# A hybrid mixer and mixture-of-experts block: modulation buffers, the zero fill, two orders of issue, and the accumulators of the tail

## The chip, the cores and the metric

The kernel runs on one core of one Trainium2 chip. The metric is the device time of one execution in microseconds (us). Before the change it is 1450.79 us, the median of 3 runs (1450.4 to 1452.89).

## The reference

One layer of a hybrid block over 512 latent tokens of width 1024 with a prefix of 256 context tokens, in float32. Cut to what matters here:

```python
sh1, sc1, g1, sh2, sc2, g2 = modulation(c, w_mod, b_mod, 6)      # silu(c) @ w_mod + b_mod
cm = modulation(c_ctx, w_mod, b_mod, 2)
hc = rmsnorm(ctx) * (1 + cm[1]) + cm[0]
hx = rmsnorm(x) * (1 + sc1) + sh1
# p = h @ w_in: retention k, v; delta-net k, v behind a conv of length 3; decays and betas ("gates"); queries
sol = triangular_solve(a + I, [beta*v, beta*exp(g)*k])            # per chunk of 128 tokens, head, direction
x = x + g1 * rmsnorm(mixer_out(retention(...), delta_net(...), ...))
h2 = rmsnorm(x) * (1 + sc2) + sh2
x = x + g2 * rmsnorm(moe(h2))                                     # 64 experts, 8 per token, and a shared one
```

The context tokens only supply the first states of the scans. In the mixture of experts each token's eight expert outputs are weighted and summed.

## The kernel before, in words

The program is written phase by phase against a framework that hands out buffers from pools, sets the semaphores, and lists the instructions of each engine; every engine then works off its own list in order, and a DMA's issue is an instruction in the list of the engine that issues it (SP for most loads). A buffer that is reused makes its next writer wait.

Float32 products are done as three matmuls of a high and a low part (`mm3`, lines 111 to 113). The high part is a cast (`hi_of`, mostly on ACT, line 100), the low part a subtraction (`lo_of`, line 107, on DVE or POOL). A unit of weights is a raw tile of 512 KB (`raw`, three buffers, line 148) and its two parts (`wu`, four buffers in a ring that `gcv` shares, so three for weights).

*Modulation (phase0, to about 64 us).* Sixteen tiles `wm` of w_mod of 512 KB each, line 300, in five buffers (three of `raw`, two of a pool of their own); matmuls into four accumulators; x and ctx normalised (POOL does x, line 286), transposed (lines 330 and 338), and turned into `hTc` and `hTx`.

*State features (phaseG, to about 350 us).* First two context projections in units of two rows of 128 (`rcA`, `rcB`, copied at line 415). At its start ACT issues a DMA that fills the DRAM buffer `zd` (1.5 MB) with zeros, from a tile of 258 columns (line 382); `zd` later receives the inverse's blocks. Then 16 columns of gates (`gT`, lines 434 and 435, transposed at line 439), and twelve convolution blocks: four of keys, four of values, four of queries, each a projection (`projT`) followed by short ACT and DVE work (lines 494 to 501). `prep(t)` builds for each of six chunks a decayed product `CT` and stores it to `cd`; two small transposes of `br` go to `bd` (lines 528 to 534). `base()` loads both back as `M` and `bb` and inverts 32 x 32 triangles on DVE, step by step. Behind the value blocks, transposes at line 717 make `vtok`.

*Retention, output projection (phaseR, phaseO), then the experts (phaseM, about 740 to 1417 us).* Each expert loads three weights of 1 MB on SP (line 1178; the last slot, a spill-over expert, by POOL gathers at line 1176), multiplies, and POOL scatters its result `y` with addition into one of two DRAM accumulators `accd[0]`, `accd[1]` (line 1258). They alternate, except that the last four slots (61 to 64) all go to `accd[1]`, which lets `accd[0]` (`m0`) and half of the block's input (`x1`) be loaded in iteration 62 of the loop. A second loop (`cnt` passes, none for these inputs) follows, then the *tail*: load `accd[1]` in four tiles, add `m0`, take the mean square (ACT), its power -0.5 (`rsqrt`: one DVE instruction, one POOL power), scale, add to the output.

Of the kernel before, what the change touches and what calls it, by code (L numbers as in the profile page):

```python
# [9 lines left out]
F32 = mybir.dt.float32  # L10
F32R = mybir.dt.float32r
# [3 lines left out]
OP = mybir.AluOpType  # L15
# [56 lines left out]
class K:  # L72
# [128 lines left out]
    def run(self, upto="end"):  # L201
        nc, tc, a = self.nc, self.tc, self.a
        main = self.main = self.pool("main")
        self.pes = ExitStack()
        self.psum = self.pool("ps", es=self.pes, space=PSUM)
        self.wi = a["w_in"][0].rearrange("(k p) n -> p k n", p=128)
        self.ident = main.tile([128, 128], F32, name="ident")
        self.mhalf = main.tile([128, 1], F32, name="mhalf")
        nc.vector.memset(self.mhalf, -0.5)
        self.vecT = main.tile([128, 68], F32, name="vecT")  # L210
        self.sc = main.tile([128, 8], F32, name="scc")
        self.keep = self.pool("keep")
        self.rawp = self.pool("raw", bufs=3)
        self.w8 = {"a": self.pool("w8a", bufs=4)}
        self.pat, self.wn, self.pre = "a", 0, {}
        self.hxs, self.gcs, self.hcs = ExitStack(), ExitStack(), ExitStack()
        self.ctx.callback(self.hxs.close)
        p = self.pool("hxp", side="right", es=self.hxs)
        self.hxpool = p
        self.hTx = p.tile([128, 8, 512], F32R, name="hTx", tag="b0")  # L220
        self.hLx = p.tile([128, 8, 512], F32R, name="hLx", tag="b1")
        self.gc = self.pool("gc", side="right", es=self.gcs)
        p = self.pool("hcp", side="right", es=self.hcs)
        self.hTc = p.tile([128, 8, 256], F32R, name="hTc")
        self.hLc = p.tile([128, 8, 256], F32R, name="hLc")
        self.phase0()
        if upto == "0":
            for s in (self.hcs, self.gcs, self.hxs, self.pes):
                s.close()
            return  # L230
        self.phaseG()
        self.phaseR()
        if upto == "R":
            self.w8s.close()
            self.hxs.close()
            self.pes.close()
            return
        self.phaseO()
        self.phaseM()


    def phase0(self):
# [50 lines left out]

        pm = [self.pa(), self.pa(), self.pa(), self.pc()]
        wv = a["w_mod"][0].rearrange("(p k) n -> p k n", k=8)
        for k in range(8):
            for hf in range(2):
                i = k * 2 + hf
                w = (self.rawp if i % 5 < 3 else wp).tile([128, 1024], F32, name="wm", tag="raw")
                nc.sync.dma_start(w, wv[:, k, hf * 1024:hf * 1024 + 1024])  # L300
                if k < 7:
                    wu = self.wt8([128, 2, 1024], F32R, "wmu")
                    wh, wl = wu[:, 0], wu[:, 1]
                    self.hi_of(wh, w, "act")
                    self.lo_of(wl, w, wh)
                for q in range(2):
                    s = slice(q * 512, q * 512 + 512)
                    o = pm[hf * 2 + q][0:2]
                    if k < 7:
                        self.mm3(o, sch[:, k], scl[:, k], wh[:, s], wl[:, s], k == 0, False)  # L310
                    else:
                        nc.tensor.matmul(o, sc[:, k], w[:, s], start=False, stop=True)
# [14 lines left out]
        for k in range(8):  # L327
            pc = self.pc()
            for t in range(2):
                nc.tensor.transpose(pc[:, t * 128:t * 128 + 128], xs[4 + t][:, k * 128:k * 128 + 128], self.ident)  # L330
            h = wp.tile([128, 256], F32, name="hc")
            nc.vector.tensor_scalar(h, pc[:, 0:256], modT[:, 8 + k, 1:2], modT[:, k, 1:2], op0=OP.mult, op1=OP.add)
            self.hi_of(self.hTc[:, k], h, "act")
            self.lo_of(self.hLc[:, k], h, self.hTc[:, k])
        for k in range(8):
            px = self.pi()
            for t in range(4):
                nc.tensor.transpose(px[:, t * 128:t * 128 + 128], xs[t][:, k * 128:k * 128 + 128], self.ident)
            h = wp.tile([128, 512], F32, name="h", tag="h")
            nc.scalar.activation(h, px, AF.Identity, scale=modT[:, 8 + k, 0:1], bias=modT[:, k, 0:1])  # L340
            self.hi_of(self.hTx[:, k], h, "pool")
            self.lo_of(self.hLx[:, k], h, self.hTx[:, k])
# [3 lines left out]
    def phaseG(self):  # L346
# [30 lines left out]

        cd_, zd, bd = dp.tile([6, 4, 16512], F32, name="cd"), dp.tile([6, 4, 16512], F32, name="zd"), dp.tile([2, 24, 128], F32, name="bd")
        gd = dp.tile([48, 128], F32, name="gd")
        zero = gp.tile([128, 258], F32, name="zero", tag="E")  # L380
        nc.gpsimd.memset(zero, 0.0)
        nc.scalar.dma_start(zd.rearrange("t h n -> (t h n)").rearrange("(p a n) -> p a n", p=128, n=258), zero[:, None, :].to_broadcast([128, 12, 258]))
        plane = lambda d, t: bass.AP(tensor=d.tensor, offset=d.offset + t * 66048, ap=[[128, 128], [16512, 4], [1, 128]])
        blocks = lambda d, t0, t1: bass.AP(tensor=d.tensor, offset=d.offset + t0 * 66048, ap=[[4128, (t1 - t0) * 16], [128, 32], [1, 32]])
        tri = gc.tile([128, 2, 128], F32, name="tri")
# [45 lines left out]

        px, pc = self.projT(2048, n=16, ctx=True)
        gT = gc.tile([16, 768], F32, name="gT", tag="vq")
        nc.scalar.copy(gT[:, 0:512], px[0:16])
        nc.scalar.copy(gT[:, 512:768], pc[0:16, 0:256])
        pt = self.pc()
        for t in range(6):
# [48 lines left out]
        nc.scalar.activation(kts, kts, AF.Exp)  # L486


        def conv(b, dx, dc):
            cv = lambda j: self.vecT[:, 24 + j * 12 + b:25 + j * 12 + b]  # L490
            r = self.projT({0: 3088, 1: 1024, 2: 1536}[b // 4] + (b % 4) * 128, ctx=dc is not None, lo="dve" if b // 4 == 1 else "pool")
            for ps, dst, n in ((r, dx, 512),) if dc is None else ((r[0], dx, 512), (r[1], dc, 256)):
                t = ctile()
                nc.scalar.activation(dst, ps[:, 0:n], AF.Identity, scale=cv(1))
# [29 lines left out]
        for l in range(2):  # L524
            nc.vector.tensor_scalar(nD[:, l], br[:, :, 4:8], even[:, l:l + 1], None, op0=OP.mult)
            stt(nD[:, l], br[:, :, 0:4], odd[:, l:l + 1], nD[:, l], op0=OP.mult, op1=OP.add)
        for dr in range(2):
            ps = self.pc()
            brd = gc.tile([128, 6, 4], F32, name="brd", bufs=2)
            nc.vector.tensor_copy(brd, br[:, :, dr * 4:dr * 4 + 4])  # L530
            nc.tensor.transpose(ps[0:24, 0:128], brd.rearrange("p t h -> p (t h)"), self.ident)
            bt = gc.tile([24, 128], F32, name="bt", bufs=2)
            nc.scalar.copy(bt, ps[0:24, 0:128])
            nc.sync.dma_start(bd[dr], bt)

        ZT, QE, CTs = {}, {}, {}

        def prep(t):
# [158 lines left out]
                        self.d("gdn_o", fl(zz), t - 2)  # L697
                    ptt(o, o, bj(c), op=OP.mult)

        for t in range(6):  # L700
            prep(t)
        gps.close()
        bps = ExitStack()
# [7 lines left out]
        vc = gcv[:, 2:4].rearrange("p a (h d) -> p (a h) d", h=2)  # L711
        for h in range(4):
            conv(8 + h, vx[:, h], vc[:, h])
        for t in range(6):
            pk = self.pc()
            for h in range(4):
# [6 lines left out]

        qx = gc.tile([128, 4, 512], F32, name="qx", tag="vq")
        for h in range(4):
            conv(h, qx[:, h], None)
        pq = self.pc()
        for h in range(4):
            sq = ctile()
# [413 lines left out]
    def phaseM(self):  # L1143
# [258 lines left out]
        for e in range(NE + 2):  # L1402
# [9 lines left out]
                convert(e + 2, 0)  # L1412
            make(e + 2, 0)
            if e > 0:
                down(aT, SL[e - 1], W[e - 1], raw(e - 1, 2), 1 if e - 1 > NE - 4 else (e - 1) % 2)
                load(e + 2, 2)
            make(e + 2, 1)
            prepare(e + 4)
            if e == NE - 2:

                halves = lambda w: [w[:, i * 1024:i * 1024 + 1024] for i in range(2)]
                m0 = halves(raw(e, 0)) + halves(raw(e, 1))
                x1 = halves(raw(e + 1, 0)) + halves(raw(e + 1, 1))
                for t in range(4):
                    nc.sync.dma_start(m0[t], self.accd[0][t * 128:t * 128 + 128])
                for t in range(2, 4):
                    nc.sync.dma_start(x1[t], self.out[t * 128:t * 128 + 128])


        cnt = nc.values_load(nx[0:1, 0:1], min_val=0, max_val=62)  # L1430
        with tc.For_i(0, cnt) as _:
# [7 lines left out]
            pgu = self.pa()  # L1439
            for n in range(2):  # L1440
                proj(pgu[:, n * 256:n * 256 + 256], [xT[:, h] for h in range(2)], w[n])
            down(turn_act(act(pgu[:, 0:256], pgu[:, 256:512])), ix, ws, raw(NE, 2), 1)


        m = halves(raw(NE, 0)) + halves(raw(NE, 1))
        r = q.tile([128, 4], F32, name="fr")
        for t in range(4):
            (nc.scalar if t % 2 else nc.sync).dma_start(m[t], self.accd[1][t * 128:t * 128 + 128])
        for t in range(4):
            tt(m[t], m[t], m0[t], op=OP.add)  # L1450
            self.d("moe", m[t], t)
            junk = q.tile([128, 1024], BF, name="xT", bufs=2)
            nc.scalar.activation(junk, m[t], AF.Square, accum_out=r[:, t:t + 1])
            self.rsqrt(r[:, t:t + 1], r[:, t:t + 1], 1.0 / D, EPS)
        for t in range(4):
            nc.vector.scalar_tensor_tensor(m[t], m[t], r[:, t:t + 1], g2p, op0=OP.mult, op1=OP.mult)
            if t < 2:
                nc.gpsimd.dma_start(self.out[t * 128:t * 128 + 128], m[t], accum_op=OP.add)
            else:
                tt(m[t], m[t], x1[t], op=OP.add)  # L1460
                (nc.scalar if t % 2 else nc.sync).dma_start(self.out[t * 128:t * 128 + 128], m[t])
        self.pes.close()

# [20 lines left out]
```

## Time and profile before

| | before |
|---|---|
| median of 3 runs | 1450.79 us |
| profiled execution | 1450.15 us, span 1448.4 us, so 1.75 us around it |
| busy share | PE 92%, DVE 62%, ACT 45%, POOL 28% |
| chain that ended last, by engine | PE 66%, DVE 8%, DMA 8%, POOL 2% |
| DMA engines by stage | full from about the middle of the span, 350 to 370 GB/s there |

The chain is followed back from the last instruction to what released it. The page also shows the span in 40 slices of 36 us; each digit is a busy share in tenths, for PEclk the clock that TensorE was granted (9 is 90% or more of 2.4 GHz, 5 is half), for DMA the mean busy share of its 16 engines:

```profile
PE   6989888899999999997799999999999999999991
PEclk9899999999999999999899999999999999999995
DMA  8643421102226578566388999999999999999954
```

TensorE has its thinner slices at the very start, between 72 and 290 us and at 650 to 725 us, and does next to nothing in the last one; the DMA engines have theirs from 72 to about 430 us.

### The profile page before, as it was taken

To read this page: it belongs to the slowest core of one execution; us is meant where nothing else is said; L and a number is where in the kernel's file an instruction comes from. 1 tells how busy PE (TensorE), PEld (TensorE's weight loads), DVE (VectorE), ACT (ScalarE), POOL (GpSimd) and SP (SyncE) were. 2 spreads that over 40 slices of the span, in tenths; PEclk is the share of its full clock that TensorE was granted. 3 is DMA by queue.
4 is the path that set the end of the run, shared out by engine and by line. 5 is a ranking of instruction groups with operands and counts; after the bars stand their busy time and mean duration, and the time that the engine had idled before them with its cause. 6 is when DMAs were issued, how large, how long until landed. Compare 5 with 4: busy or idle time off the path is not lost.

```text
span 1448.4 us, 20720 instructions
## 1 busy us (share of the span) xinstructions
PE 1338.8 (92%) x7848; PEld 1085.2 (75%) x7848; DVE 901.3 (62%) x1268; ACT 655.7 (45%) x927; POOL 404.1 (28%) x330
## 2 busy tenths in 40 slices
PE   6989888899999999997799999999999999999991
PEld 2668776898887767776678787878787878888770
DVE  5635695566777556557366666666666666666543
ACT  5534442543323223244145655555555555555531
POOL 0414644855330000012022222222222222223312
PEclk9899999999999999999899999999999999999995
DMA  8643421102226578566388999999999999999954
GB/s 283 191 106 107 125 58 41 44 16 84 78 69 203 177 212 232 167 248 245 136 282 295 351 364 347 367 354 347 364 357 361 362 362 357 368 353 353 327 184 124
DMA packets 138841, 340.51 MB, mean 235 GB/s; under 512 B 28218, under 2 KB 84574, under 8 KB 113780
## 3 DMA queue, kind: packets, MB, share of 16 engines
q1 hardware_dynamic: 110952, 289.46, 56.5%
q0 software_dynamic: 19584, 38.99, 10.7%
q10 hardware_dynamic: 8204, 10.72, 2.4%
q8 instruction: 63, 1.03, 0.3%
q14 instruction: 38, 0.31, 0.1%
HBM read 326.59 MB, written 48.31 MB: 259 GB/s over the span
## 4 chain that ended last, share of the span: by engine, by line
PE 66%; DVE 8%; DMA 8%; POOL 2%; issue 2%; ACT 1%; SPq 0%; ACTq 0%; DVEq 0%; POOLq 0%
PE cs L1253 15%; PE acc L113 12%; PE acc L112 12%; PE acc L111 12%; PE ci L1222 4%; DMA raw<-in_w_in_dram 2%; PE ci L1056 2%; DMA wd<-in_w_down_dram 2%; DVE wu L107 1%; PE acc L1242 1%; PE acc L1067 1%; DMA mraw<-in_w_mod_dram 1%; ACT wu L100 1%; PE ci L596 1%; PE cs L655 1%
## 5 line engine op out<-in xcount | busy, mean ns | idle before, releaser
L111 PE MATMUL acc<-wh,xT 128*128 128x256 f32 x1040 | 304.9, 293 | 0.0
L113 PE MATMUL acc<-wh,xT 128*128 128x256 f32 x1040 | 294.4, 283 | 0.0
L112 PE MATMUL acc<-wl,xT 128*128 128x256 f32 x1040 | 294.1, 283 | 0.0
L1158 DVE TENSOR_TENSOR wl<-w,wh 128x2048 fp32r<-128x2048 f32 x88 | 201.6, 2291 | 87.4 <-PE acc L112 86.0
L1253 PE MATMUL cs<-wd,aT 128*128 128x512 f32 x520 | 235.8, 596 | 2.9 <-DMA wd<-in_w_down_dram 2.1
L1258 POOL DMA_INDIRECT acc<-y,slots x64 | 101.9, 1592 | 474.7 <-ACT y L1255 427.4
L1156 ACT CAST wh<-w 128x2048 fp32r<-128x2048 f32 x88 | 167.3, 1901 | 100.7 <-PE acc L113 85.6
L111 PEld LDWEIGHTS acc<-wh,xT 128*128 128x128 f32 x1040 | 199.6, 192 | 0.2 <-issue 0.2
L112 PEld LDWEIGHTS acc<-wl,xT 128*128 128x128 f32 x1040 | 199.4, 192 | 0.2 <-issue 0.2
L113 PEld LDWEIGHTS acc<-wh,xT 128*128 128x128 f32 x1040 | 198.8, 191 | 0.0
L1253 PEld LDWEIGHTS cs<-wd,aT 128*128 128x128 f32 x520 | 94.5, 192 | 97.6 <-issue 96.6
L1225 DVE TENSOR_TENSOR xT<-ci,xT 128x512 fp32r<-128x512 f32 x130 | 89.1, 686 | 89.7 <-ACT xT L1224 89.6
L100 ACT CAST wu<-raw 128x1024 fp32r<-128x1024 f32 (+1 forms) x73 | 74.9, 1036 | 113.4 <-DMA raw<-in_w_in_dram 74.1
L1158 DVE TENSOR_TENSOR wl<-wgu,wh 128x2048 fp32r<-128x2048 f32 x42 | 96.3, 2292 | 41.5 <-PE acc L112 41.4
L111 PE MATMUL acc<-hTx,wu 128*128 128x512 f32 (+1 forms) x296 | 119.2, 403 | 1.9 <-ACT wu L100 1.9
L113 PE MATMUL acc<-hTx,wu 128*128 128x512 f32 (+1 forms) x296 | 118.4, 400 | 1.5 <-DVE wu L107 1.5
L112 PE MATMUL acc<-hLx,wu 128*128 128x512 f32 (+1 forms) x296 | 117.9, 398 | 0.0
L107 DVE TENSOR_TENSOR wu<-raw,wu 128x1024 fp32r<-128x1024 f32 (+1 forms) x61 | 77.1, 1270 | 64.6 <-ACT wu L100 63.5
L1156 ACT CAST wh<-wgu 128x2048 fp32r<-128x2048 f32 x42 | 79.7, 1898 | 50.0 <-PE acc L113 42.1
L1222 PEld LDWEIGHTS ci<-ident,xg 128*128 128x128 f32 x520 | 73.4, 192 | 29.8 <-issue 29.5
L1214 POOL DMA_INDIRECT xg<-h2d,slots x64 | 71.3, 1113 | 31.6 <-issue 18.0
L1222 PE MATMUL ci<-ident,xg 128*128 128x128 f32 x520 | 80.0, 278 | 0.0
(492 smaller groups left out, 2371.6 us busy)
## 6 DMA issues: line engine op xcount, KB each, us to landing
wd<-in_w_down_dram SPq DMA_DIRECT2D x64, 1024.0 KB
w<-in_w_gate_dram SPq DMA_DIRECT2D x43, 1024.0 KB
w<-in_w_up_dram SPq DMA_DIRECT2D x43, 1024.0 KB
raw<-in_w_in_dram SPq DMA_DIRECT2D x56, 512.0 KB
wgu<-in_w_gate_dram SPq DMA_DIRECT2D x21, 1024.0 KB
wgu<-in_w_up_dram SPq DMA_DIRECT2D x21, 1024.0 KB
mraw<-in_w_mod_dram SPq DMA_DIRECT2D x32, 512.0 KB
wm<-in_w_mod_dram SPq DMA_DIRECT2D x16, 512.0 KB
```

Of the source, the lines that this page charges most:

```text
L100: nc.scalar.copy(dst, src)
L107: (self.nc.gpsimd if eng == "pool" else self.nc.vector).tensor_tensor(dst, src, hi.bitcast(F32), op=OP.subtract)
L111: mm(out, ah, bh, start=start, stop=False)
L112: mm(out, ah, bl, start=False, stop=False)
L113: mm(out, al, bh, start=False, stop=stop)
L1156: nc.scalar.copy(h[:, i:i + max(n, 1024)], w[:, i:i + max(n, 1024)])
L1158: eng(l[:, i:i + n], w[:, i:i + n], h[:, i:i + n].bitcast(F32), op=OP.subtract)
L1214: nc.gpsimd.indirect_dma_start(xg[:, :], None, self.h2d[:, :], bass.IndirectOffsetOnAxis(ap=ix, axis=0), bounds_check=511, oob_is_err=False)
L1222: nc.tensor.transpose(ps[:, k * 128:k * 128 + 128], xv[:, :, c * 4 + k], self.ident)
L1225: tt(l, ps, h.bitcast(F32), op=OP.subtract)
L1253: nc.tensor.matmul(ps, aT[:, m], wd[:, s], start=k == 0, stop=k == 1)
L1258: nc.gpsimd.indirect_dma_start(self.accd[acc][:, :], bass.IndirectOffsetOnAxis(ap=sx, axis=0), y[:, :], None, bounds_check=511, oob_is_err ...
```

## The change

Five parts.

1. Modulation weights: tiles 3 to 10 get eight buffers in the space that `hTx` and `hLx` take later; the others use the three `raw` buffers; the pool of two is used for them no more.
2. Zero fill: the source is now 774 columns of `gcv`, set to zero on POOL, so a packet has 3096 bytes instead of 1032; the DMA is issued on ACT right behind the first copy of `gT`.
3. `prep(0)` and `prep(1)` come ahead of the two transposes of `br`.
4. The projection of the first query block comes ahead of the transposes to `vtok`.
5. Tail: scatters alternate to the end, extra passes go to `accd[0]`; `accd[1]` is loaded in iteration 64 (`m1`) and x1 with it, `accd[0]` at the end; the last root is a bias on ACT (a constant tile `eps`) and a power on POOL.

```diff
@@ -209,0 +210,2 @@
+        self.eps = main.tile([128, 1], F32, name="eps")
+        nc.vector.memset(self.eps, EPS)
@@ -220,2 +221,0 @@
-        self.hTx = p.tile([128, 8, 512], F32R, name="hTx", tag="b0")
-        self.hLx = p.tile([128, 8, 512], F32R, name="hLx", tag="b1")
@@ -295,0 +296 @@
+        wms = [t[:, i] for t in [self.hxpool.tile([128, 4, 1024], F32, name="wm", tag=tag) for tag in ("b0", "b1")] for i in range(4)]
@@ -299 +300 @@
-                w = (self.rawp if i % 5 < 3 else wp).tile([128, 1024], F32, name="wm", tag="raw")
+                w = wms[i - 3] if 3 <= i < 11 else self.rawp.tile([128, 1024], F32, name="wm", tag="raw")
@@ -334,0 +336,2 @@
+        self.hTx = self.hxpool.tile([128, 8, 512], F32R, name="hTx", tag="b0")
+        self.hLx = self.hxpool.tile([128, 8, 512], F32R, name="hLx", tag="b1")
@@ -380 +383 @@
-        zero = gp.tile([128, 258], F32, name="zero", tag="E")
+        zero = gcv[:, 2:4].rearrange("p a n -> p (a n)")[:, 0:774]
@@ -382 +384,0 @@
-        nc.scalar.dma_start(zd.rearrange("t h n -> (t h n)").rearrange("(p a n) -> p a n", p=128, n=258), zero[:, None, :].to_broadcast([128, 12, 258]))
@@ -434 +436,2 @@
-        nc.scalar.copy(gT[:, 0:512], px[0:16])
+        with tc.issue_after(nc.scalar.copy(gT[:, 0:512], px[0:16]).ins):
+            nc.scalar.dma_start(zd.rearrange("t h n -> (t h n)").rearrange("(p a n) -> p a n", p=128, n=774), zero[:, None, :].to_broadcast([128, 4, 774]))
@@ -489 +492,4 @@
-        def conv(b, dx, dc):
+        def conv_in(b, ctx):
+            return self.projT({0: 3088, 1: 1024, 2: 1536}[b // 4] + (b % 4) * 128, ctx=ctx, lo="dve" if b // 4 == 1 else "pool")
+
+        def conv(b, dx, dc, r=None):
@@ -491 +497,2 @@
-            r = self.projT({0: 3088, 1: 1024, 2: 1536}[b // 4] + (b % 4) * 128, ctx=dc is not None, lo="dve" if b // 4 == 1 else "pool")
+            if r is None:
+                r = conv_in(b, dc is not None)
@@ -527,9 +533,0 @@
-        for dr in range(2):
-            ps = self.pc()
-            brd = gc.tile([128, 6, 4], F32, name="brd", bufs=2)
-            nc.vector.tensor_copy(brd, br[:, :, dr * 4:dr * 4 + 4])
-            nc.tensor.transpose(ps[0:24, 0:128], brd.rearrange("p t h -> p (t h)"), self.ident)
-            bt = gc.tile([24, 128], F32, name="bt", bufs=2)
-            nc.scalar.copy(bt, ps[0:24, 0:128])
-            nc.sync.dma_start(bd[dr], bt)
-
@@ -700 +698,11 @@
-        for t in range(6):
+        prep(0)
+        prep(1)
+        for dr in range(2):
+            ps = self.pc()
+            brd = gc.tile([128, 6, 4], F32, name="brd", bufs=2)
+            nc.vector.tensor_copy(brd, br[:, :, dr * 4:dr * 4 + 4])
+            nc.tensor.transpose(ps[0:24, 0:128], brd.rearrange("p t h -> p (t h)"), self.ident)
+            bt = gc.tile([24, 128], F32, name="bt", bufs=2)
+            nc.scalar.copy(bt, ps[0:24, 0:128])
+            nc.sync.dma_start(bd[dr], bt)
+        for t in range(2, 6):
@@ -713,0 +722 @@
+        q0 = conv_in(0, False)
@@ -726 +735 @@
-            conv(h, qx[:, h], None)
+            conv(h, qx[:, h], None, q0 if h == 0 else None)
@@ -1415 +1424 @@
-                down(aT, SL[e - 1], W[e - 1], raw(e - 1, 2), 1 if e - 1 > NE - 4 else (e - 1) % 2)
+                down(aT, SL[e - 1], W[e - 1], raw(e - 1, 2), (e - 1) % 2)
@@ -1419 +1428 @@
-            if e == NE - 2:
+            if e == NE:
@@ -1422,4 +1431,2 @@
-                m0 = halves(raw(e, 0)) + halves(raw(e, 1))
-                x1 = halves(raw(e + 1, 0)) + halves(raw(e + 1, 1))
-                for t in range(4):
-                    nc.sync.dma_start(m0[t], self.accd[0][t * 128:t * 128 + 128])
+                m1 = halves(raw(e - 2, 0)) + halves(raw(e - 2, 1))
+                x1 = halves(raw(e - 1, 0))
@@ -1427 +1434,3 @@
-                    nc.sync.dma_start(x1[t], self.out[t * 128:t * 128 + 128])
+                    nc.sync.dma_start(x1[t - 2], self.out[t * 128:t * 128 + 128])
+                for t in range(4):
+                    nc.sync.dma_start(m1[t], self.accd[1][t * 128:t * 128 + 128])
@@ -1442 +1451 @@
-            down(turn_act(act(pgu[:, 0:256], pgu[:, 256:512])), ix, ws, raw(NE, 2), 1)
+            down(turn_act(act(pgu[:, 0:256], pgu[:, 256:512])), ix, ws, raw(NE, 2), 0)
@@ -1448 +1457 @@
-            (nc.scalar if t % 2 else nc.sync).dma_start(m[t], self.accd[1][t * 128:t * 128 + 128])
+            (nc.scalar if t % 2 else nc.sync).dma_start(m[t], self.accd[0][t * 128:t * 128 + 128])
@@ -1450 +1459 @@
-            tt(m[t], m[t], m0[t], op=OP.add)
+            tt(m[t], m[t], m1[t], op=OP.add)
@@ -1453,2 +1462,4 @@
-            nc.scalar.activation(junk, m[t], AF.Square, accum_out=r[:, t:t + 1])
-            self.rsqrt(r[:, t:t + 1], r[:, t:t + 1], 1.0 / D, EPS)
+
+            nc.scalar.activation(junk, m[t], AF.Square, scale=D ** -0.5, accum_out=r[:, t:t + 1])
+            nc.scalar.activation(r[:, t:t + 1], r[:, t:t + 1], AF.Identity, bias=self.eps)
+            nc.gpsimd.tensor_tensor(r[:, t:t + 1], r[:, t:t + 1], self.mhalf, op=OP.pow)
@@ -1460 +1471 @@
-                tt(m[t], m[t], x1[t], op=OP.add)
+                tt(m[t], m[t], x1[t - 2], op=OP.add)
```

What this does to the lists of the engines, at three places.

ACT's list from the first units of weights (`wu`) to the gate copies (`gT`); `zd` is the buffer filled with zeros, `rcA` and `rcB` are context projections. Before:

```order
L100 CAST wu<-raw 128x1024 x2
L382 DMA zd<-zero 1536x1x258
L415 COPY rcA<-acc 128x512 x2
L100 CAST wu<-raw 128x1024 x2
L100 CAST wu<-raw 128x128
L415 COPY rcB<-acc 128x512 x2
L434 COPY gT<-acc 16x512
L435 COPY gT<-acc 16x256
```

and now:

```order
L100 CAST wu<-raw 128x1024 x2
L417 COPY rcA<-acc 128x512 x2
L100 CAST wu<-raw 128x1024 x2
L100 CAST wu<-raw 128x128
L100 CAST wu<-raw 128x1024
L417 COPY rcB<-acc 128x512 x2
L100 CAST wu<-raw 128x1024
L436 COPY gT<-acc 16x512
L437 DMA zd<-gcv 512x1x774
L438 COPY gT<-acc 16x256
```

The DMA to `zd` moved from ahead of the copies of `rcA` to between the two gate copies, and two casts of weights come ahead of the gates.

POOL's list at the end of the preparation: `QE3` to `QE5` are decay factors of the last chunks, `W` the inverse's work area, `wu_1597` (now `wu_1592`) the weights of a value convolution. Before:

```order
L550 TENSOR_TENSOR QE3_1231<-QE3_1231,rk_1083 128x512
L565 MEMSET W_1296 96x2048
L550 TENSOR_TENSOR QE4_1250<-QE4_1250,rk_1083 128x512
L550 TENSOR_TENSOR QE5_1269<-QE5_1269,rk_1083 128x512
L568 MEMSET W_1296 96x32 x2
L107 TENSOR_TENSOR wu_1597<-raw_1595,wu_1597 128x512 x2
```

and now:

```order
L548 TENSOR_TENSOR QE3_1226<-QE3_1226,rk_1078 128x512
L107 TENSOR_TENSOR wu_1592<-raw_1590,wu_1592 128x512 x2
L563 MEMSET W_1291 96x2048
L548 TENSOR_TENSOR QE4_1245<-QE4_1245,rk_1078 128x512
L548 TENSOR_TENSOR QE5_1264<-QE5_1264,rk_1078 128x512
L566 MEMSET W_1291 96x32 x2
```

The weight's two halves (x2) moved ahead of the memset of `W` and of the last two decay products.

SP's list at the end of the program: `wd` are down-projection weights, `wgu<-acc` and `w<-acc` loads of an accumulator, `w<-out_dram` loads of x; the branches are the second loop. Before:

```order
L1178 DMA wd<-in_w_down_dram 128x2048 x3
L1425 DMA wgu<-acc_4923 128x1024 x4
L1427 DMA w<-out_dram 128x1024 x2
L1431 COMPARE_AND_BRANCH
L1431 UNCONDITIONAL_BRANCH x2
L1479 BRANCH_PREFETCH_HINT
L1431 REGISTER_ALU
L1431 COMPARE_AND_BRANCH
L1431 UNCONDITIONAL_BRANCH
L1448 DMA w<-acc_4924 128x1024 x2
```

and now:

```order
L1187 DMA wd<-in_w_down_dram 128x2048 x2
L1434 DMA w<-out_dram 128x1024 x2
L1187 DMA wd<-in_w_down_dram 128x2048
L1436 DMA wgu<-acc_4919 128x1024 x3
L1440 COMPARE_AND_BRANCH
L1440 UNCONDITIONAL_BRANCH x2
L1490 BRANCH_PREFETCH_HINT
L1440 REGISTER_ALU
L1440 COMPARE_AND_BRANCH
L1440 UNCONDITIONAL_BRANCH
L1436 DMA wgu<-acc_4919 128x1024
L1457 DMA w<-acc_4918 128x1024 x2
```

Before, all four loads of `accd[0]` and then x stand behind the weights. Now x stands ahead of the last of them, three loads of `accd[1]` behind it and one behind the loop, ahead of the loads of `accd[0]`.

## Rows read from the trace of the kernel before

**Rows 1.** Waits, 5 to 41 us. Columns: waiter, what it waited for, total us, times, longest.
```profile
ACT wmu L100 <- DMA wm<-in_w_mod_dram: 9.0, 9, 4.1
ACT junk L282 <- DMA x<-in_x_dram: 3.2, 1, 3.2
```

**Rows 2.** Busy time by engine in two stretches: us (x instructions), granted clock, DMA share, GB/s.
```profile
13.40:40.00 26.60, 25.59 (x92) 7.79 (x92) 16.43 (x16) 14.64 (x20) 0.92 (x2) 1.00 0.88 311
48.00:52.00 4.00, 3.96 (x15) 3.46 (x16) 3.48 (x7) 3.45 (x6) 1.24 (x2) 0.50 0.42 120
```

**Rows 3.** Waits, 40 to 110 us, TensorE for the normalised x.
```profile
PE ci L338 <- POOL x L286: 2.0, 3, 0.7
```

**Rows 4.** Timeline of ACT: start, us, engine, line, operation, [idle before <-releaser].
```profile
63.51 0.59 ACTq L382 DMA_DIRECT2D zd<-zero  x1
77.14 1.24 ACT L100 CAST wu<-raw 128x1024 fp32r<-128x1024 f32 x2 [10.06 <-DMA raw<-in_w_in_dram]
```

**Rows 5.** Timeline of PE around the stall at 73 to 84 us.
```profile
73.36 0.40 PE L112 MATMUL acc<-wu,hTc 128*128 128x512 f32 x1
73.59 0.40 PE L113 MATMUL acc<-wu,hLc 128*128 128x512 f32 x1
78.24 0.80 PE L111 MATMUL acc<-wu,hTc 128*128 128x512 f32 x1 [4.25 <-ACT wu L100]
83.93 0.47 PE L113 MATMUL acc<-wu,hLc 128*128 128x512 f32 x1
```

**Rows 6.** Busy time by engine in four stretches.
```profile
66.00:72.00 6.00, 6.00 (x28) 4.82 (x27) 1.86 (x2) 1.05 (x1) 0.00 (x0) 1.00 1.11 214
78.00:84.00 6.00, 5.30 (x12) 3.87 (x13) 1.43 (x2) 0.97 (x3) 1.04 (x1) 0.50 0.58 156
86.00:96.00 10.00, 9.76 (x62) 6.46 (x63) 2.86 (x10) 0.57 (x1) 2.23 (x3) 1.00 0.00 0
100.00:130.00 30.00, 30.00 (x168) 25.84 (x169) 16.95 (x36) 13.40 (x23) 7.54 (x6) 1.00 0.51 141
```

**Rows 7.** Timeline of PE, around the gate transposes.
```profile
97.61 0.54 PE L439 MATMUL cs<-ident,gT 16*128 16x16 f32 x6 [0.45 <-ACT gT L435]
98.56 0.50 PE L111 MATMUL acc<-hTx,wu 128*128 128x512 f32 x1 [0.41 <-ACT wu L100]
```

**Rows 8.** Timeline of POOL, end of the preparation.
```profile
163.31 1.80 POOL L565 MEMSET W<- 96x2048 f32 x1 [3.04 <-DVE QE L548]
167.20 5.07 POOL L107 TENSOR_TENSOR wu<-raw,wu 128x512 fp32r<-128x512 f32 x4
```

**Rows 9.** Timeline of ACT, the casts of the weights of the convolutions there.
```profile
166.07 1.04 ACT L100 CAST wu<-raw 128x1024 fp32r<-128x1024 f32 x1
```

**Rows 10.** Waits, 176 to 243 us.
```profile
DVE N L569 <- DMA M<-cd: 1.8, 1, 1.8
DVE rq L129 <- POOL rq L127: 4.0, 1, 4.0
PE cs L717 <- ACT gcv L501: 4.2, 1, 4.2
```

**Rows 11.** Timeline of SP's queue, the loads of the tail.
```profile
1392.04 1.75 SPq L1425 DMA_DIRECT2D wgu<-acc  x4
```

**Rows 12.** Timeline of POOL, the last scatters.
```profile
1392.94 1.00 POOL L1176 DMA_INDIRECT wd<-in_w_down_dram,wi  x1 [5.96 <-PE cs L1253]
1394.24 1.58 POOL L1258 DMA_INDIRECT acc<-y,slots  x1 [0.30 <-issue]
1405.79 1.56 POOL L1258 DMA_INDIRECT acc<-y,slots  x1 [9.96 <-DMA acc<-y,slots]
```

**Rows 13.** The chain that ended last, in order of time: start, us, what.
```profile
1412.93 4.73 DMA acc<-y,slots
1418.48 4.50 DMA acc<-y,sl_i
1424.30 7.97 DMA w<-acc
```

## What the change is predicted to do

> **What bounds the kernel now.** I read the share of the chain and the forty slices first (the table above): TensorE is the bound nearly everywhere, so a change pays where TensorE idles or runs at half clock, and costs where it is made to wait. Then the waits and the stretches by window, stage by stage, and for the places that the diff touches the timelines.
>
> *Modulation, 3 to 48 us.* ACT waits nine times for tiles of w_mod, 9.0 us in all, and once 3.2 us for x [rows 1]. Yet TensorE is busy 25.59 of 26.60 us between 13.4 and 40 us [rows 2]: most of ACT's waits lie beside a TensorE that is behind anyway. Afterwards TensorE waits three times for a normalised x, 2.0 us [rows 3], and at 48 to 52 us it still runs at clock 0.50 [rows 2].
>
> *The stall at 74 us.* The zero fill leaves ACT's queue at 63.51; the cast at 77.14 then waits 10.06 us for its weights [rows 4]. DMA is full meanwhile (1.11) but moves only 214 GB/s [rows 6]. TensorE starts matmuls every 0.23 us up to 73.59, idles 4.25 us and works off the next twelve at clock 0.50; the last of them starts at 83.93 [rows 5, 6]. From 86 to 96 us the DMA engines are idle (0.00) and TensorE goes on from weights already on chip [rows 6].
>
> *The triangular inverse, 176 to 243 us.* It begins when M has landed (DVE waited 1.8 us for it), and is a fixed list on DVE, which idles chiefly 4.0 us for POOL's power of rq; TensorE's one long wait there, 4.2 us, lies beside DVE's work [rows 10].
>
> *The tail.* The last two scatters go to one accumulator, so the second waits for the first: 4.73 and 4.50 us, then four loads of 0.5 MB take 7.97 us [rows 13].
>
> **The change part by part.** All against the profiled execution's own 1450.15 us (span 1448.4 and 1.75 around it); the median of the runs shown is 0.64 us higher, 1450.79, and I add that at the end.
>
> **Buffers for w_mod.** The loads run eleven tiles ahead instead of five. The SP list has x's first tile two w_mod tiles earlier; the last two w_mod tiles still wait for a raw buffer, with the other three x behind them, but find an idle DMA. TensorE's own 1.0 us of idleness (26.60 less 25.59) can go, and the 2.0 us on x for the greater part; the two overlap, as the transposes of x are filled in wherever the modulation ends. I take -2.0. Ends: +0.5, if POOL's memset, now ahead of x's normalisation, waits for its buffer and holds x back; -5, if without these gaps the clock does not fall and the 3.96 us of work at half clock [rows 2] shrink by half, with 1.0 more beside it.
>
> **Zero fill.** Behind the gate copies it lies in the stretch without any DMA traffic. The transfer itself is then hidden by the gate and first key matmuls. Undisturbed, the last of the twelve would start at 73.59 + 12 x 0.23 = 76.4 instead of 83.93: -7.5, of which 4.25 is the stall and the rest the clock. I take -7.5; ends -8.5 (neighbouring short gaps too) and -4.25 (the clock falls anyway). What must be late next: the weights of the next convolutions; but one of these feeds TensorE for some 8 us (168 matmuls in 100 to 130 us without a gap [rows 6]), while 0.5 MB needs 2.4 us even at 214 GB/s. Larger packets count nothing by themselves, as nobody waits for the fill; it is read back only after the inverse.
>
> **Gate transposes.** In the new TensorE list some matmuls of the first key convolution stand ahead of them, so the gaps of 0.45 and 0.41 us [rows 7] are covered: -0.9 (0 to -1.1). The stretch behind is full (30.00 of 30 us [rows 6]), so what is won so far, -10.4, is carried through it.
>
> **Order around the preparation.** On POOL two halves of a convolution's weight split move ahead of the memset of W and of the last two decay products. Four such halves take 5.07 us, so two take 2.5 us; POOL was idle 3.04 us just before the memset [rows 8], so between nothing and 2.5 is added before M: I take the middle, +1.2. Ends: -1.5, since one load less runs beside M's transfer, and +2.5. The moved transposes of br and their two small stores on SP come before M's source is complete, and cost nothing.
>
> **Query projection early.** It fills TensorE's 4.2 us wait [rows 10], but DVE holds the end of that stage and its list is the same: 0. Ends -4.0 (the power of rq comes early enough to remove DVE's wait) and +1 (one accumulator bank is held longer).
>
> **Tail.** The final scatter now goes to the other accumulator and need not wait for the one before: y is ready some 0.9 us before its start at 1418.48. But three loads of the odd accumulator (1.5 MB) start beside it when the last odd scatter has landed. What such company costs: the scatter at 1394.24 held the next one until 1405.79, 11.5 us against 4.7, beside a gather of 1 MB, four loads of the even accumulator (2 MB) and two of the output (1 MB, queued right behind them) [rows 11 to 13]. That is 6.9 us for 4 MB, or 2.6 for 1.5 MB; less 0.9 makes +1.7. One load more than before is left for the end: 7.97 / 4 = +2.0. Before, the loads for this lay under the experts' matmuls, which is the cover now gone. The new rsqrt moves one short instruction from DVE to ACT: 0 (-0.5 to +1). The tail together +3.7; ends -1 (scatter and loads don't disturb each other, the extra load hides) and +9 (the scatter as slow as at 1394.24, 6.9 - 0.9 + 2.0 = 8.0, and the rsqrt).
>
> The scatter and its neighbours share the DMA engines, and 11.5 against 4.7 us is what that did here. The Trainium skill, page "DMA: Bandwidth & Descriptors", section "Queues, rings and completion order", says that each engine takes turns between the queues that have work for it, packet by packet. By that, one other queue can at most double the scatter's time: +4.5 and not +2.6, so a tail of +5.6 and a total 1.9 us later, 1447.2. The trace agrees that queues share, but its factor of 2.4 is more than double; there POOL's gather stood ahead in the scatter's own queue as well.
>
> Sum: -2.0 - 7.5 - 0.9 + 1.2 + 0 + 3.7 = -5.5, so 1444.65 for the profiled execution and 1445.3 as a median.
>
> **Rivals.**
> *More is won (1440).* The clock stays up in the modulation (-3 more) and DVE's 4.0 us wait partly goes with the earlier projection (-2). For it: both gaps are real waits. Against it: in both places another engine is nearly full.
> *The tail takes it (1449.6).* Scatter and loads collide as at 1394.24: tail 8.0, which is 4.3 more. For it: that very row. Against it: less than half the bytes.
> *The stall only moves, so the change doesn't do what it says (1452.8).* The fill meets other loads and TensorE stalls for 7.5 us there. Against it: the empty DMA at 86 to 96 us.
> *Slower: the preparation is held up by ACT's cast (1456.7).* POOL's two moved halves wait for a cast that stood at 166.07 [rows 9]. If that cast can't come earlier, because its weight buffer or its data is not free, the memset moves from 163.31 to 166.07 + 1.04 + 2.5 = 169.6, 6.3 us; the exponentials of the last two chunks stand behind the same cast on ACT, and the products behind them on POOL, so up to as much again, 12.6. With -10.4 before it and +3.7 in the tail that ends at +5.9. It makes the kernel slower from a delay of 9.6 us; between 6.3 and that the result is no change. For it: engines run their lists in order. Against it: the load is issued long before, and the row shows no wait.
>
> **How the numbers follow.** A difference under 0.2%, 2.9 us, can't be told from no change. Forecast 0.50, own range 1442 to 1447.6; more won 0.24; tail 0.10; stall moves, or a hold-up below 9.6 us, 0.08; slower 0.08. Faster: 0.50 + 0.24 + 0.04 from the better part of the tail case = 0.78; same 0.14; slower 0.08. From 1438.5 to 1450.0 lie the forecast, most of more won and nearly all of the tail case, about 0.8.
>
> **What would show it.** Right: no wait of TensorE between 66 and 86 us and clock 1.00 there; the fill's transfer at some 84 to 96 us; M's transfer issued 9 us earlier than before (-10.4 + 1.2); the last scatter slower than 4.5 us and more than 8 us for the loads behind it. Wrong: a wait for raw anywhere in 86 to 140 us, M less than 5 us earlier, an inverse longer than 67 us, or a tail that ends sooner after the last y than before.

## The result, and the profile after

The changed kernel takes 1440.47 us (median of 4 runs, 1438.03 to 1441.17), the kernel before beside it 1450.60 us (4 runs); the ratio is 0.9925 with a 95% interval of 0.9908 to 0.9943. Run again later, beside the last experiments, it stood at 0.9945 (0.9930 to 0.9960). The forecast was 1445.3 us, 5.5 us less than before; the gain is about twice that in the first comparison and 8 us in the second. The time lies 1.5 us below the forecast's own range of 1442 to 1447.6.

Where the two profiled executions part (the start of an event in each, in us, and how much earlier it is in the changed kernel):

| event | before | after | moved | forecast |
|---|---|---|---|---|
| M's load issued on SP | 170.34 | 163.23 | -7.1 | -9.2 |
| first scatter of an expert | 755.61 | 747.62 | -8.0 | -9.2 |
| scatter of the 60th slot | 1373.56 | 1361.87 | -11.7 | -9.2 |
| y of the last slot ready | 1417.40 | 1403.99 | -13.4 | -9.2 |
| end of the span | 1448.4 | 1439.4 | -9.0 | -5.5 |

Up to the experts the kernel gains a little less than forecast, but this is rough: another execution with the same code up to there (the tail alone, below) has its first scatter at 749.79 and not 755.61; in the experts, whose matmuls the diff doesn't touch, 5.4 us come on top (13.4 less 8.0), and there the pace is steady; in the tail 4.4 are given back (13.4 less 9.0).

*Modulation.* SP's queue, the loads of x before, then the changed kernel (start, us, queue, line, operation, count):

```profile
30.84 2.13 SPq L260 DMA_DIRECT2D x<-in_x_dram  x4
```

```profile
22.40 0.33 SPq L260 DMA_DIRECT2D x<-in_x_dram  x1
31.23 1.61 SPq L301 DMA_DIRECT2D wm<-in_w_mod_dram  x2
32.89 1.37 SPq L260 DMA_DIRECT2D x<-in_x_dram  x3
```

ACT's squares of x there:

```profile
32.59 1.06 ACT L282 ACTIVATE junk<-x 128x1024 bf16<-128x1024 f32 x1
...
39.80 1.06 ACT L282 ACTIVATE junk<-x 128x1024 bf16<-128x1024 f32 x1 [1.38 <-DMA x<-in_x_dram]
```

TensorE's wait for the normalised x in the changed kernel, 40 to 110 us, and the stretch of 44 to 48 us (columns as in [rows 2]), before and after:

```profile
PE ci L341 <- POOL x L286: 1.9, 3, 0.7
```

```profile
44.00:48.00 4.00, 2.70 (x12) 1.62 (x10) 3.44 (x11) 3.00 (x6) 3.52 (x4) 0.50 0.12 43
44.00:48.00 4.00, 2.66 (x12) 1.71 (x10) 3.52 (x9) 2.63 (x6) 3.27 (x4) 0.50 0.15 54
```

Only the first tile of x comes earlier. The last two w_mod tiles still wait for a `raw` buffer until 31.23, and three of the four x tiles are queued behind them on SP. The wait of [rows 3] is the same, 1.9 us against 2.0, and the clock still falls to 0.50.

*The zero fill.* The stretches of [rows 6] in the changed kernel, with the one between:

```profile
66.00:72.00 6.00, 6.00 (x28) 4.97 (x27) 2.59 (x3) 1.74 (x3) 0.00 (x0) 1.00 0.73 183
72.00:78.00 6.00, 5.42 (x29) 4.22 (x28) 1.69 (x3) 3.18 (x4) 2.46 (x3) 1.00 0.88 222
78.00:84.00 6.00, 6.00 (x39) 3.94 (x38) 4.59 (x11) 0.00 (x0) 2.41 (x2) 1.00 0.49 128
```

```profile
86.00:96.00 10.00, 10.00 (x65) 8.23 (x64) 3.56 (x15) 4.63 (x9) 0.00 (x0) 1.00 0.50 180
```

The stall of 4.25 us is gone: TensorE's one wait left between 66 and 86 us is 0.6 us, for POOL and not for a DMA. The clock stays at 1.00 (0.50 before), and from 86 to 96 us, where no DMA ran, the fill and a few loads now move 180 GB/s beside a TensorE that is busy all the time.

*Preparation and inverse.* POOL's last but one decay factor (`E`) ahead of the memset, before and after, then the end of the preparation in the changed kernel, and SP's load of M there:

```profile
153.97 1.37 POOL L547 TENSOR_TENSOR E<-rcB,g 128x512 f32<-128x512 f32 x1 [1.46 <-DVE QE L548]
```

```profile
144.00 1.37 POOL L545 TENSOR_TENSOR E<-rcB,g 128x512 f32<-128x512 f32 x1 [1.88 <-DVE QE L546]
...
152.02 3.00 POOL L107 TENSOR_TENSOR wu<-raw,wu 128x512 fp32r<-128x512 f32 x2 [2.15 <-ACT wu L100]
156.29 1.81 POOL L563 MEMSET W<- 96x2048 f32 x1 [1.27 <-DVE QE L546]
```

```profile
163.23 0.34 SPq L559 DMA_DIRECT2D M<-cd  x1
```

The two halves stand where [rows 8] had none. That decay factor starts 10.0 us earlier than before, but the memset only 7.0 and M's load 7.1: from the factor to M's load it takes 19.2 us instead of 16.4. From M's load to the end of the inverse it takes 71.5 us, before 72.4. DVE's wait for the power of rq is unchanged [rows 10]:

```profile
DVE rq L129 <- POOL rq L127: 4.0, 1, 4.0
```

*The experts.* POOL's scatters seven experts apart, before and after:

```profile
1007.83 1.59 POOL L1258 DMA_INDIRECT acc<-y,slots  x1 [7.39 <-ACT y L1255]
...
1080.06 1.59 POOL L1258 DMA_INDIRECT acc<-y,slots  x1 [7.38 <-ACT y L1255]
```

```profile
1007.92 1.59 POOL L1267 DMA_INDIRECT acc<-y,slots  x1 [7.26 <-ACT y L1264]
...
1079.27 1.59 POOL L1267 DMA_INDIRECT acc<-y,slots  x1 [7.25 <-ACT y L1264]
```

72.23 and 71.35 us for seven, 10.32 and 10.19 for one. TensorE is full in both. Its instructions and their order are the same; the matmuls themselves stand closer.

*The tail.* The chain that ended last, to set beside [rows 13]:

```profile
1399.52 4.79 DMA acc<-y,slots
1404.32 0.33 SPq L1436
1404.69 1.45 SPq L1436
1406.19 6.19 DMA wgu<-acc
1413.01 0.34 ACTq L1457
1413.39 7.19 DMA w<-acc
1420.67 2.37 DVE w L1459 x2
1423.07 2.19 ACT xT L1463 x4
```

The last scatter is issued at 1404.26, 0.3 us behind its y (before, 1.1), and lands after 6.9 us (its row of DMA issues; the last figure is us to landing):

```profile
acc<-y,sl_i POOLq DMA_INDIRECT x1, 6.9
```

The three loads beside it land later still, 1406.19 + 6.19 = 1412.38, and only then does the first load of `accd[0]` leave, at 1413.0. At the branch of the second loop SP waits for the scatter and then for these loads (waiter, what it waited for, total us, times, longest):

```profile
SPq L1440 <- DMA acc<-y,sl_i: 4.2, 1, 4.2
SPq L1440 <- DMA wgu<-acc: 0.9, 1, 0.9
```

From the scatter's issue to that first load it is 8.7 us; before it was 5.4. Behind the loop DVE can add one tile early and the other three only from 1420.67 on:

```profile
1417.73 1.23 DVE L1459 TENSOR_TENSOR w<-w,wgu 128x1024 f32<-128x1024 f32 x1 [15.40 <-DMA w<-acc]
1420.67 3.50 DVE L1459 TENSOR_TENSOR w<-w,wgu 128x1024 f32<-128x1024 f32 x3 [1.71 <-DMA w<-acc]
```

So the sums and squares that had filled the gaps between landings follow one another.

### The profile page after: what moved, and what is told of

Read it like the earlier page. It is cut to its first block, busy times and chain, and to the rows that moved or that the text cites. A ratio compares the mean times of both kernels' runs of the same rounds, so it can differ in the third digit from the quotient of the medians.

```text
span 1439.4 us, 20721 instructions
## 1 busy us (share of the span) xinstructions
PE 1327.0 (92%) x7848; PEld 1076.2 (75%) x7848; DVE 906.0 (63%) x1265; ACT 655.4 (46%) x931; POOL 403.8 (28%) x330
## 4 chain that ended last, share of the span: by engine, by line
PE 62%; DMA 10%; DVE 9%; issue 4%; POOL 3%; ACT 2%; SPq 0%; DVEq 0%; ACTq 0%; POOLq 0%
PE cs L1262 14%; PE acc L113 11%; PE acc L111 11%; PE acc L112 11%; PE ci L1231 4%; PE ci L1065 2%; DMA w<-in_w_up_dram 2%; DMA raw<-in_w_in_dram 2%; DMA w<-in_w_gate_dram 2%; DVE wu L107 1%; PE acc L1251 1%; PE acc L1076 1%; DMA mraw<-in_w_mod_dram 1%; ACT wu L100 1%; POOL wu L107 1%
## 5 line engine op out<-in xcount | busy, mean ns | idle before, releaser
L111 PE MATMUL acc<-wh,xT 128*128 128x256 f32 x1040 | 302.1, 291 | 0.0
L113 PE MATMUL acc<-wh,xT 128*128 128x256 f32 x1040 | 291.1, 280 | 0.0
L112 PE MATMUL acc<-wl,xT 128*128 128x256 f32 x1040 | 290.8, 280 | 0.0
L111 PEld LDWEIGHTS acc<-wh,xT 128*128 128x128 f32 x1040 | 197.1, 190 | 0.2 <-issue 0.2
L112 PEld LDWEIGHTS acc<-wl,xT 128*128 128x128 f32 x1040 | 196.5, 189 | 0.2 <-issue 0.2
L113 PEld LDWEIGHTS acc<-wh,xT 128*128 128x128 f32 x1040 | 196.0, 188 | 0.0
```

Source lines behind the costliest of these rows:

```text
L111: mm(out, ah, bh, start=start, stop=False)
L112: mm(out, ah, bl, start=False, stop=False)
L113: mm(out, al, bh, start=False, stop=stop)
```

## The experiments

Each is timed beside the kernel before on the same chip; a ratio is to that. The kernel before was 1446.8 to 1447.9 us in these.

**Where do the experts' 5.4 us come from?** Only the accumulators of the last slots differ there. But a tile `eps` is now allocated ahead of most others, so that they lie 32 bytes higher: `wh` begins at byte 75136 of each partition before and 75168 after, in the built programs.

The kernel before with such a tile and nothing else:

```diff
         nc.vector.memset(self.mhalf, -0.5)
+        nc.vector.memset(main.tile([128, 8], F32, name="pad"), 0.0)
```

> The kernel before with one unused 32-byte tile (set to zero once) in the place where the change has the tile eps, so that every buffer behind it lies 32 bytes higher; nothing else. In the trace of the changed kernel an expert takes 10.19 us instead of 10.32 and the starts of the experts' matmuls stand 0.1205 us apart instead of 0.1233. Theory A, the place in memory does it: this kernel shows 10.19 us per expert and is 5 to 8 us faster than before (some 54 experts at 0.13 us, and 4 ns in each earlier matmul whose moving operand lies there). Rival B, the experts' pace comes with another part of the change (the alternating accumulators) or from the run: 10.32 us per expert and no change (within 1 us).

Ratio 0.9971 (0.9961 to 0.9981), -4.2 us. Seven experts take 71.36 us:

```profile
1003.14 1.59 POOL L1259 DMA_INDIRECT acc<-y,slots  x1 [7.26 <-ACT y L1256]
...
1074.50 1.59 POOL L1259 DMA_INDIRECT acc<-y,slots  x1 [7.26 <-ACT y L1256]
```

And the changed kernel without the shift:

```diff
-        self.mhalf = main.tile([128, 1], F32, name="mhalf")
-        self.eps = main.tile([128, 1], F32, name="eps")
+        mh = main.tile([128, 2], F32, name="mhalf")
+        self.mhalf, self.eps = mh[:, 0:1], mh[:, 1:2]
```

> The changed kernel with eps as the second column of the tile that holds -0.5, so that all buffers lie where they lay before; nothing else. Theory A: 10.32 us per expert, 5 to 7 us slower than the changed kernel, so about 1446 us, which is what the five parts of the change give without it. Rival B: 10.19 us per expert and 1440.5 us as the changed kernel.

Ratio 0.9983 (0.9971 to 0.9995), 1444.74 us, and 72.24 us for seven experts:

```profile
1000.23 1.59 POOL L1267 DMA_INDIRECT acc<-y,slots  x1 [7.39 <-ACT y L1264]
...
1072.47 1.59 POOL L1267 DMA_INDIRECT acc<-y,slots  x1 [7.38 <-ACT y L1264]
```

Theory A holds in both directions: the pace comes with the 32 bytes and goes with them. Some 50 experts at 0.127 us would be 6.3 us; 4.2 arrive (2.7 to 5.6). Part of the rest is that TensorE, now faster, waits longer for the last weights (4.6 us for `wd` in `b_shift32`, 4.1 in the changed kernel, 2.1 before). Without the shift the five parts together give 2.5 us (0.7 to 4.2).

Which places are good? The kernel before with 64 bytes (`[128, 16]` in the same line):

> The kernel before with an unused tile of 64 bytes, so that the buffers behind it lie 64 bytes higher and not 32. The 32-byte shift gave 10.193 us per expert against 10.320, with matmul starts 0.1205 against 0.1233 us apart. Theory, a moving operand that begins at a multiple of 64 bytes is the slow case: 10.32 us and no change. Rival, only multiples of 128 are slow: 10.19 us and 4 us faster, as with 32 bytes.

Neither theory holds: ratio 0.9981 (0.9970 to 0.9993), and 10.245 us per expert, between the two. Then, at the other end of memory, on top of the changed kernel with the old tail (`a_oldtail` below):

```diff
+        nc.vector.memset(self.pool("padr", side="right").tile([128, 16], F32, name="padr"), 0.0)
         self.ctx.callback(self.hxs.close)
```

> The changed kernel with the old tail and an unused tile of 64 bytes at the other end of memory, which puts hTx and hLx (moving operands of the projections) from 96 to 32 bytes past a multiple of 128, the place at which weights were read fastest (matmul starts 0.2287 us apart instead of 0.2333). Theory, it is the moving operand's own place that counts: the key convolutions show 0.229 us between starts instead of 0.233, and the kernel is 2 to 4 us faster than the one with the old tail alone (0.9915 of before), so 0.9885 to 0.990. Rival, it is the place of the operands relative to each other or something else: 0.233 stays and the time is that of the old tail alone, or the experts lose their 10.193 us.

Ratio 0.9939 (0.9923 to 0.9955). The key convolutions do come to 0.227 us between starts, but the experts fall back to 10.33, though their weights lie where they were fast:

```profile
999.21 1.59 POOL L1268 DMA_INDIRECT acc<-y,slots  x1 [7.39 <-ACT y L1265]
...
1071.54 1.59 POOL L1268 DMA_INDIRECT acc<-y,slots  x1 [7.41 <-ACT y L1265]
```

The same with 8 columns, 32 bytes:

> The same with a tile of 32 bytes: hTx and hLx lie 64 bytes past a multiple of 128. Theory of the moving operand's own place: 0.2333 us between starts as at 64 bytes in the earlier run for weights, and the time of the old tail alone, 0.9915 of before within 0.0015. Rival: 0.229 here and not with 64 bytes.

Ratio 0.9922 (0.9907 to 0.9937): experts at 10.19, key convolutions at 0.233. The theory that the moving operand's own place decides has fallen; see the last section.

**The fill alone** (the two hunks on `zero` and `gT` of the diff):

> The kernel before with the zero fill alone moved (from gcv, larger packets, behind the first gate copy). Prediction: the stall of 4.25 us and the half clock behind it go, -7.5 us, and with the order of the gate copies up to -8.4: about 1442.5 us. Rival, the loads of the first projections are late for themselves and the stall stays in part: -3 to -5 us.

Ratio 0.9941 (0.9925 to 0.9957), -8.5 us (-10.9 to -6.2). The prediction's mechanism and size: between 72 and 84 us the clock is 1.00 and TensorE nearly full. The run moves the fill and makes its packets larger at once; whether larger packets in the old place would have shortened the stall too was not tried.

```profile
72.00:78.00 6.00, 5.66 (x25) 4.23 (x23) 2.65 (x3) 3.19 (x5) 1.02 (x1) 1.00 0.45 122
78.00:84.00 6.00, 5.83 (x41) 4.60 (x42) 3.92 (x8) 1.33 (x2) 3.86 (x4) 1.00 0.86 208
```

**The buffers for w_mod alone** (the hunks on `hTx`, `wms` and `wm`):

> The kernel before with the eight more buffers for the modulation weights alone. Prediction's term: -2.0 us (0.5 to -5). By the trace of the changed kernel, where TensorE still waits 1.9 us for the normalised x and the modulation's result is only 0.45 us earlier: -0.5 to -1, which can't be told from no change.

Ratio 1.0000 (0.9987 to 1.0012). TensorE waits as long for x as before:

```profile
PE ci L339 <- POOL x L284: 2.2, 3, 1.0
```

**The two orders alone** (the hunks on `conv_in`, `prep` and `q0`):

> The kernel before with the two changes of order alone (two preparations ahead of the transposes of br; first query projection ahead of the value transposes). Prediction's terms: +1.2 for the preparation (-1.5 to 2.5), 0 for the projection (-4 to 1), so about +1 us, M's transfer issued at about 171.5 us instead of 170.34 and the inverse 72 us long as before. Rival, the hold-up on POOL is larger: M at 174 us or later, +4 us.

Ratio 0.9992 (0.9981 to 1.0004), no change that can be told. M is issued where expected, 1.2 us later than before:

```profile
153.38 1.37 POOL L542 TENSOR_TENSOR E<-rcB,g 128x512 f32<-128x512 f32 x1 [1.46 <-DVE QE L543]
```

```profile
171.53 0.34 SPq L556 DMA_DIRECT2D M<-cd  x1
```

That it hits the 171.5 so well is luck: the decay factor is 0.6 us earlier in this execution (153.38), and from there to M's load it takes 18.2 us instead of 16.4, 1.8 more.

**The tail.** The kernel before with the new accumulators and tail alone, no tile moved:

> The kernel before with the alternating accumulators and the new tail alone; eps lies beside the constant -0.5, so no buffer moves. Prediction's term: +3.7 us (-1 to 9); by the two traces, last y to end 35.4 against 31.0 us: +4.4. Rival, the earlier end of the last experts pays it back: within 1 us of before.

Ratio 1.0031 (1.0019 to 1.0043), +4.5 us. And the changed kernel with the old tail (the last two hunks undone):

> The changed kernel with the accumulators and the tail of the kernel before (the tile eps stays in its place). By the prediction's term the new tail costs 3.7 us; by the two traces, from the last y to the end 35.4 us against 31.0, 4.4 us. Theory: this kernel is 3 to 5 us faster than the changed one, about 1436 us. Rival, the longer tail is paid back by the earlier end of the experts (no loads of accumulators beside them): no change or slower, 1440 to 1442 us.

Ratio 0.9915 (0.9902 to 0.9928), 1433.92 us. It was not timed beside the changed kernel, whose two ratios are 0.9925 and 0.9945; by those it is 1 to 4 us faster, and by its own profile the tail takes 29.8 us from the last y instead of 35.4. It is the fastest version of all here, and beats both kernels by median.

Do loads and scatter slow each other, or is the scatter slow for itself? All loads of the odd accumulator behind the loop, by a swap of tiles:

```diff
-                m1 = halves(raw(e - 2, 0)) + halves(raw(e - 2, 1))
+                m = halves(raw(e - 2, 0)) + halves(raw(e - 2, 1))
-                for t in range(4):
-                    nc.sync.dma_start(m1[t], self.accd[1][t * 128:t * 128 + 128])
...
-        m = halves(raw(NE, 0)) + halves(raw(NE, 1))
+        m1 = halves(raw(NE, 0)) + halves(raw(NE, 1))
...
             (nc.scalar if t % 2 else nc.sync).dma_start(m[t], self.accd[0][t * 128:t * 128 + 128])
+            (nc.scalar if t % 2 else nc.sync).dma_start(m1[t], self.accd[1][t * 128:t * 128 + 128])
```

> The changed kernel with all four loads of the odd accumulator behind the second loop (in the tiles of the last slot; the even accumulator goes into the older tiles), so that the last scatter has no loads beside it. Theory: in the changed kernel the scatter and the three loads slow each other, 8.7 us from the scatter's issue to the first load behind the loop, which waits for both. Here that stretch is 4.5 to 5.5 us, as in the kernel before, and the eight loads (4 MB) then take 12 to 14 us instead of 7.2: in all 1 to 4 us slower than the changed kernel, since what the scatter gains is lost on the loads. Rival, the scatter into the other accumulator is slow for itself: the stretch stays at 8 us or more.

The scatter alone takes 4.70 us, the loads 11.0 from SP's last issue of one:

```profile
1401.53 4.70 DMA acc<-y,sl_i
...
1408.49 11.00 DMA w<-acc
```

So they do slow each other, 6.9 against 4.7 us. The eight loads take 12.3 us from the first issue on SP, at 1407.17, to the last landing, within the 12 to 14 expected (the five of the changed kernel 7.6, from 1413.01 to 1420.58). But the whole is not slower: 0.9932 (0.9916 to 0.9948) against 0.9945 of the changed kernel beside it:

> The changed kernel once more, beside the others of this batch. Its first runs stood at 0.9925 of before. Expected 0.990 to 0.994 and 10.193 us per expert; it is the measure for the other three.

The changed kernel came out just above what was expected of it there. Last y to end is 33.6 us here, 35.9 there. What the expectation missed comes behind the last landing, 15.4 us here and 18.8 there: two tiles are added while the other two are still being loaded.

```profile
1414.47 2.36 DVE L1458 TENSOR_TENSOR wgu<-wgu,w 128x1024 f32<-128x1024 f32 x2 [14.87 <-DMA w<-acc]
1419.52 2.36 DVE L1458 TENSOR_TENSOR wgu<-wgu,w 128x1024 f32<-128x1024 f32 x2 [2.68 <-DMA w<-acc]
```

Loading the odd accumulator early, beside the scatter, wins nothing that shows.

## Why the prediction was right, and where not

The direction, the main term and the sum of the tail were right; the total came out larger through a term that was not in the sum. That it came out so clearly faster is in part luck: without that term the change gives 2.5 us (0.7 to 4.2), less than the 2.9 us under which the forecast itself saw no change. By its steps:

1. *Zero fill and gate transposes, -8.4:* measured -8.5 (-10.9 to -6.2). The stall, the clock behind it, and the cover at 86 to 96 us all as described.
2. *Buffers for w_mod, -2.0:* nothing, within 1.8 us. The step that failed is "the 2.0 us on x for the greater part". The text had seen that three x tiles stand behind the last two w_mod tiles on SP and took it that an idle DMA would make up for it; but their issue is late (32.89 us; before, all four went out from 30.84 on), and TensorE waits 1.9 and 2.2 us for x in the two runs against 2.0. No run issued x earlier, so that the order on SP is what holds x back is argued and not shown. By the profiles the first projection matmul starts at 46.6 to 49.9 us in the eight executions with the buffers and at 47.4 to 49.3 in the six without.
3. *Preparation and projection, +1.2 and 0:* -1.2 with 1.7 either way in time. The preparation's term was too small: from the decay factor to M's load 1.8 us were added by the order alone and 2.9 in the changed kernel. With 10.0 won ahead of it, where 10.4 was forecast, that makes M's 7.1 instead of 9.2. These sizes are rough, as M's issue differs by up to 2.0 us between executions with the same early code (163.23 in the changed kernel, 161.23 with the old tail). What offsets it in the time is not shown.
4. *Tail, +3.7:* +4.5 (2.8 to 6.2). The scatter beside three loads takes 2.4 us more (6.9 against 4.5), where the term had 2.6, and it starts 0.8 sooner behind its y, where the term had 0.9. The +2.0 for the loads behind it was wrong: the five of them take 7.2 us (8.3 in the run with the tail alone), the four before took 8.0. In its place come two costs that the prediction lacks: the loop's branch waits for the three loads too, another 1.2 us to 1412.4 that no one needs them for (with the tail alone the scatter itself, at 8.0 us, came last), and from the last landing to the end it takes 18.7 us instead of 16.1, since the work stands behind tiles that land together. That the sum agrees is in part luck.

   The Trainium skill's turns between queues ("DMA: Bandwidth & Descriptors", "Queues, rings and completion order") gave an estimate of +4.5 for the scatter as a bound. In the kernels with the new tail it took 6.5 to 8.0 us against 4.5 to 4.7 alone: it stays under that bound, and the row of the trace was the better estimate.
5. *The tile eps, not in the sum:* -4.2. The section on the change names it, and the prediction gave it no term. It moved the buffers, and the experts' matmuls with them. This is what the forecast lacks. Without it the five parts together give -2.5 (-0.7 to -4.2); timed one by one they add up to -8.5 + 0 - 1.2 + 4.5 = -5.2. The intervals of the four, about 2 us each way, allow for both, so where the 2.7 us between lie is open.

Of the rivals, "more is won" names the measured time and has the wrong cause: the clock at 44 to 48 us still falls to 0.50 and DVE still waits 4.0 us. The stall did not move. ACT's cast held up the preparation only a little: POOL waited 2.15 us for it, and M lost 2.9 us there, not 6.3 or more.

## What to carry to other kernels

A bulk transfer that nobody waits for belongs where the trace shows the DMA engines idle; here its gain (the stall and the clock behind it), read from rows as 8.4 us, was measured as 8.5 (6.2 to 10.9). More buffers for one stream did not help here, where the load that came late (x) still stood behind two loads that waited for a buffer; look for that in the queue's list first. A loop that makes no pass can still wait for the loads ahead of it (here 1.2 us). And when a diff allocates even one small tile, compare the same matmuls' spacing before and after before crediting the edit: undoing the shift alone tells the two apart.

## What the runs showed of the hardware that was not expected

The distance between the starts of the same matmuls depends on where the program's buffers lie: an expert takes 1.2 to 1.4% longer in the slow cases, and the starts of the key convolutions stand up to 2.8% further apart. Bytes past a multiple of 128 (from the built programs); us per expert from 48 scatters; for the key convolutions the mean distance of some 50 neighbouring starts. "Moving" marks the second operand of the matmul; `xT` and `wu` are the first:

| kernel | `wh`, `wl` (moving) | `xT` | us per expert | `hTx` (moving) | `wu` | us between starts |
|---|---|---|---|---|---|---|
| before | 0 | 0 | 10.320 | 96 | 0 | 0.2335 |
| 32 bytes | 32 | 0 | 10.193 | 96 | 32 | 0.2326 |
| 64 bytes | 64 | 0 | 10.245 | 96 | 64 | 0.2332 |
| right end 64 | 32 | 64 | 10.332 | 32 | 32 | 0.2272 |
| right end 32 | 32 | 96 | 10.193 | 64 | 32 | 0.2331 |

Over some 100 starts (85 to 145 us) the five rows have 0.2335, 0.2322, 0.2333, 0.2279 and 0.2333, and the changed kernel, with the places of the second row, 0.2311; so only the fourth row stands clear. The 10.193 at the bottom is a mean: three experts take 10.14 to 10.15 us each and the next three 10.24 to 10.25, over and over, while the changed kernel has 10.18 to 10.20 for each.

Neither operand's place alone explains it: `wh` at 32 is fast with `xT` at 0 or 96 and slow with 64. Equal places are fast for the convolutions (32 and 32) and slow for the experts (0 and 0). Buffers that other engines use at the same time moved as well in each of these, so a rule is left open.
